# Blocked inverses in a gated-delta encoder: rows of 16 by substitution, one more level by products, and the heads' pieces placed anew

## The chip, the core and the metric

One Trainium2 chip, one of its cores. The metric is the device time of one execution, in microseconds (us), as the median of several runs. TensorE (PE) multiplies, VectorE (DVE), ScalarE (ACT) and GpSimd (POOL) do the elementwise work, and SyncE (SP) issues nearly all DMAs. Each engine takes its own instructions in the order in which the program queued them.

## What is computed

A layer of an encoder on 512 tokens of width 1024. Its input projection has 72 blocks of 128 columns and a small one. Eight heads of width 128 go through a gated delta rule, forwards and backwards, in chunks of 64 tokens (the kernel takes 128 tokens with the same result). What concerns the change is the inverse of a unit lower triangular matrix for each chunk and the lengths of q:

```python
q = _l2norm(q.reshape(bsz, t, N_HEADS, HEAD_DIM)) * (HEAD_DIM ** -0.5)
...
lmat = jnp.where(strict, jnp.einsum('nbhcd,nbhsd->nbhcs', kb, k) * decay, 0.0)
eye = jnp.eye(CHUNK, dtype=lmat.dtype)
tmat = lax.linalg.triangular_solve(lmat + eye, jnp.broadcast_to(eye, lmat.shape),
                                   left_side=True, lower=True, unit_diagonal=True)
u = jnp.einsum('nbhcs,nbhsd->nbhcd', tmat, v * beta[..., None])
w = jnp.einsum('nbhcs,nbhsd->nbhcd', tmat, kb * jnp.exp(gc)[..., None])
```

Then come a scan over the chunks, a norm and gate of its output, a short convolution branch, output projections, a layer norm, a feed-forward part (1024 to 4096 and back) and a second layer norm.

## The kernel before

All large products are made three times in fp32r (high by high, high by low, low by high), so each weight block is split first: ACT copies the high part (L122), DVE subtracts it for the low part (L118).

**Slots.** The middle of the kernel (L735 to L762) is nine slots. A slot is a run of block steps; one block step is three 128x512 products of a projection (L156 to L158), and eight of them are a block. Slots 0 to 8 have 88, 48, 48, 48, 48, 48, 40, 40 and 8 block steps. Between the block steps the pieces of three heads are queued: the scan of head h-1 (`scan_end`, at the block steps in FAR), the second part of head h's local work (`local`, at MID, in slot 0 MID0) and the first part of head h+1's (at BEGIN, in slot 0 BEGIN1; head 0 itself at BEGIN0). A negative number in BEGIN counts from the slot's end. A piece runs from one `yield` to the next. Within a block step the order is scan, second part, first part, then the three products. CONV, SC and Z tell after how many steps the convolution's copy, its two taps (L344, L345) and its silu are queued. PE, DVE, ACT and POOL keep this order exactly; DMAs on SP are placed by the framework's own ordering.

**A head's local work** (`gdn_local`, L423): `grow`, the running sums of the decay, is fetched; eight DVE instructions (L431) and two exponentials (L434, L435) make the decay; DVE scales it (L446); ACT and DVE split q and k (L451, L453). POOL squares q (L457, `q2`) and multiplies q into the decay (L460). DVE transposes `q2` in blocks of 32 (L465), adds it up (L467), and five small DMAs (L469, L472) with one more reduction (L543) bring the squared lengths of q onto the tokens. PE makes the score products `pg` (L481) and DVE multiplies in the decay (L485); ACT and DVE cut out the diagonal blocks of 32 (L495, L496), `dg`. Those go to DRAM (`xd`, L499) and back, spread by rows over four partitions: four DMAs for `Nb` (L503), four for `X` (L505). PE transposes v (`pv`, L511), POOL scales it.

**The substitution** (L520 to L536) runs on POOL alone: two instructions fold each second row into its neighbour (L526, L527), then 15 steps of one product (L532) and two sums (L535), and the identity is added (L536). Four DMAs write `xo` (L538), one reads it back as `U` (L542). DVE and ACT lay out the 32-blocks' inverses (`mt`, L549 to L552), and `level` (L554) makes from them the inverses of 64 and of 128: two rounds of small products on 32x32 or 64x64 tiles of the array (`pxa`, `pya`, `pxb`, `pyb`, L563 and L575) with copies by ACT and DVE between them.

Products of the projections take turns in two PSUM banks ("m"). A block's bank comes free when DVE has done both taps on it.

## Time and profile before

| | us |
|---|---|
| median of 3 runs | 1095.07 (1091.77 to 1096.57) |
| span of the profiled execution | 1085.6 |
| median less that span | 9.5 |
| PE, DVE, ACT, POOL busy | 1021.6, 543.5, 443.5, 393.0 |
| 0 to 31.1: loads, first block, gates | 31.1 |
| slot 0 / slot 1 / slots 2 to 5 | 87.4 / 48.2 / 220.9 |
| slot 6 / slot 7 | 49.9 / 42.8 |
| slot 8 and all that follows it | 605.3 |

The profiler's execution has no time of its own beside its span. What lies around the span is taken as the 9.5 us by which the median exceeds it. A slot's ends are the starts of its first and of the next slot's first 128x512 product. Slots 1, 2, 3 and 4 begin at 118.5, 166.7, 221.3 and 275.5 us.

In a row on a stretch the first number after its ends is its length; busy us (with instructions) of PE, PEld, DVE, ACT and POOL follow, then the granted clock of TensorE as a share of 2.4 GHz (it has two levels, 1.2 and 2.4 GHz, so 0.93 is full speed for 86% of the stretch), the DMA engines' busy share and GB/s. The other rows name an instruction by the engine, the line of the kernel and the tile that it writes. "Idle before" is how long its engine stood still just ahead of it, and what ended that.

### The profile page before, as it was taken

To read this page: it belongs to the slowest core of one execution; us is meant where nothing else is said; L and a number is where in the kernel's file an instruction comes from. 1 tells how busy PE (TensorE), PEld (TensorE's weight loads), DVE (VectorE), ACT (ScalarE), POOL (GpSimd) and SP (SyncE) were. 2 spreads that over 40 slices of the span, in tenths; PEclk is the share of its full clock that TensorE was granted. 3 is DMA by queue.
4 is the path that set the end of the run, shared out by engine and by line. 5 is a ranking of instruction groups with operands and counts; after the bars stand their busy time and mean duration, and the time that the engine had idled before them with its cause. 6 is when DMAs were issued, how large, how long until landed. Compare 5 with 4: busy or idle time off the path is not lost.

```text
span 1085.6 us, 14685 instructions
## 1 busy us (share of the span) xinstructions
PE 1021.6 (94%) x5523; PEld 843.0 (78%) x5523; DVE 543.5 (50%) x919; ACT 443.5 (41%) x804; POOL 393.0 (36%) x702
## 2 busy tenths in 40 slices
PE   9798999898979797999999999989999999999996
PEld 6576878686858686878888888879888888888885
DVE  6694686676666666353322246491222233333336
ACT  5652556464636364362434233222333343323231
POOL 1156757575656566740132012064222220000005
PEclk9899999898989898999999999999999999999998
DMA  6432243333323332222326324312322333232312
GB/s 207 116 93 68 87 96 100 83 93 78 99 69 108 69 107 75 82 88 78 98 98 225 102 83 152 117 47 90 98 97 95 99 116 114 86 106 87 106 48 77
DMA packets 77750, 106.84 MB, mean 98 GB/s; under 512 B 44336, under 2 KB 53104, under 8 KB 77680
## 3 DMA queue, kind: packets, MB, share of 16 engines
q1 hardware_dynamic: 77248, 105.26, 31.9%
q8 instruction: 43, 0.70, 0.3%
q10 hardware_dynamic: 432, 0.66, 0.2%
q14 instruction: 27, 0.22, 0.1%
HBM read 101.60 MB, written 4.29 MB: 98 GB/s over the span
## 4 chain that ended last, share of the span: by engine, by line
PE 56%; POOL 15%; DVE 12%; DMA 9%; issue 4%; SPq 3%; ACT 1%; POOLq 0%; DVEq 0%
PE accd L862 16%; POOL X L535 8%; PE ps_up L157 5%; POOL xt L532 5%; PE ps_up L158 5%; PE ps_up L156 5%; PE ps_in L156 4%; PE ps_in L158 4%; PE ps_in L157 4%; PE acco L862 3%; DMA xd<-dg 2%; DMA U<-xo 2%; DMA Nb<-xd 1%; PE psup L909 1%; DVE wl_in L118 1%
## 5 line engine op out<-in xcount | busy, mean ns | idle before, releaser
L156 PE MATMUL ps_in<-xh,wh_in 128*128 128x512 f32 x576 | 241.4, 419 | 22.0 <-DVE y L345 16.7
L158 PE MATMUL ps_in<-xh,wl_in 128*128 128x512 f32 x576 | 230.4, 400 | 4.2 <-DVE wl_in L118 4.2
L157 PE MATMUL ps_in<-xl,wh_in 128*128 128x512 f32 x576 | 229.5, 398 | 0.0
L156 PEld LDWEIGHTS ps_in<-xh,wh_in 128*128 128x128 f32 x576 | 111.4, 193 | 44.2 <-issue 18.3
L158 PEld LDWEIGHTS ps_in<-xh,wl_in 128*128 128x128 f32 x576 | 110.7, 192 | 31.9 <-DVE wl_in L118 7.7
L118 DVE TENSOR_TENSOR wl_in<-raw_in,wh_in 128x1024 fp32r<-128x1024 f32 x70 | 92.3, 1318 | 81.9 <-ACT wh_in L122 77.5
L157 PEld LDWEIGHTS ps_in<-xl,wh_in 128*128 128x128 f32 x576 | 111.6, 194 | 18.5 <-issue 0.3
L122 ACT ACTIVATE wh_in<-raw_in 128x1024 fp32r<-128x1024 f32 x70 | 73.9, 1055 | 64.8 <-PE ps_in L157 55.9
L862 PE MATMUL accd<-wh_down,hh 128*128 128x512 f32 x256 | 99.6, 390 | 0.0
L862 PE MATMUL accd<-wh_down,hl 128*128 128x512 f32 x256 | 99.4, 389 | 0.0
L862 PE MATMUL accd<-wl_down,hh 128*128 128x512 f32 x256 | 99.4, 389 | 0.0
L118 DVE TENSOR_TENSOR wl_up<-raw_up,wh_up 128x1024 fp32r<-128x1024 f32 x30 | 36.8, 1225 | 121.5 <-ACT wh_up L122 121.5
L535 POOL TENSOR_TENSOR X<-X,xt 128x60 f32<-128x60 f32 (+10 forms) x240 | 88.4, 368 | 18.8
L916 POOL TENSOR_TENSOR hf<-r 128x512 f32<-128x512 f32 x32 | 46.3, 1447 | 118.6 <-ACT r L914 118.6
L156 PE MATMUL ps_up<-x1h,wh_up 128*128 128x512 f32 x224 | 87.1, 389 | 0.0
L157 PE MATMUL ps_up<-x1l,wh_up 128*128 128x512 f32 x224 | 87.1, 389 | 0.0
L158 PE MATMUL ps_up<-x1h,wl_up 128*128 128x512 f32 x224 | 87.1, 389 | 0.0
L122 ACT ACTIVATE wh_up<-raw_up 128x1024 fp32r<-128x1024 f32 x30 | 31.8, 1060 | 106.3 <-PE ps_up L157 98.7
L966 POOL TENSOR_TENSOR xs<-xs,ln_g 128x1024 f32<-128x1024 f32 (+2 forms) x4 | 7.0, 1749 | 164.9 <-ACT xs L965 164.9
L104 DVE TENSOR_TENSOR wl_down<-raw_down,wh_down 128x1024 fp32r<-128x1024 f32 x32 | 40.0, 1253 | 50.4 <-ACT wh_down L103 48.8
L532 POOL TENSOR_TENSOR xt<-X,Nb 128x120 f32<-128x120 f32 (+10 forms) x120 | 58.4, 487 | 9.3
L862 PEld LDWEIGHTS accd<-wh_down,hh 128*128 128x128 f32 x256 | 48.0, 188 | 10.4 <-ACT wh_down L103 0.4
(256 smaller groups left out, 1922.3 us busy)
## 6 DMA issues: line engine op xcount, KB each, us to landing
...
```

Of the source, the lines that this page charges most:

```text
L104: (lo_eng or nc.vector).tensor_tensor(out=lo, in0=src, in1=hi.bitcast(F32), op=ALU.subtract)
L118: (nc.gpsimd if pool else nc.vector).tensor_tensor(out=wl, in0=raw, in1=wh.bitcast(F32), op=ALU.subtract)
L122: act(out=wh, in_=raw, func=AF.Copy)
L156: nc.tensor.matmul(acc, wh[:, c], mh[k], start=(k == 0), stop=False)
L157: nc.tensor.matmul(acc, wh[:, c], ml[k], start=False, stop=False)
L158: nc.tensor.matmul(acc, wl[:, c], mh[k], start=False, stop=(k == KT - 1))
L532: sub(out=t, in0=X[:, 0:r, k:k + 2].unsqueeze(3).broadcast_to([Q, r, 2, n]), in1=Nb[:, k:k + 2, k + 1:32].unsqueeze(1).broadcast_to([Q, r, ...
L535: sub(out=X[:, 0:r, k + 1:32], in0=X[:, 0:r, k + 1:32], in1=t[:, :, m], op=ALU.add)
L862: nc.tensor.matmul(acc[:, o], a[:, ts_], b[:, hs], start=start and j == 0, stop=stop and j == 2, skip_group_check=True)
L909: nc.tensor.matmul(acc[:, ts_], a[:, c], b[k][:, ts_], start=(k == 0 and t2 == 0 and j == 0), stop=(k == KT - 1 and t2 == 1 and j == 2), s ...
L916: nc.gpsimd.tensor_tensor(out=hfl, in0=r, in1=r, op=ALU.mult)
L966: nc.gpsimd.tensor_tensor(out=y[:, js], in0=y[:, js], in1=lnc["g"][:, js], op=ALU.mult)
```

## The change

The substitution goes on blocks of 16 instead of 32. Sixty-four blocks of 16 per head are spread over 128 partitions, two to a block. `X` starts from the identity by a copy on POOL (`eye`, loaded once) instead of four DMAs; the steps are eight, on at most 16 columns, in two pieces instead of sixteen. `xo` is two fixed DRAM tiles that are zeroed once. A new level on TensorE makes the 32-blocks' inverses: `UT` on DVE, 32 products 32x32 (`px0`), a copy on ACT (`lx0`), 32 products (`py0`), and one DVE instruction that adds their right half where the mask `uppr` is one. The squares of q are made by ACT, and their sums by four products with a column of ones (`pl`) in the piece of v's transposes; the DVE transposes and reductions and the five DMAs for them go. All lists of places are new.

```diff
-BEGIN0 = (5, 6, 7, 8, 8, 9, 11, 12, 15, 15, 16, 18, 18, 20, 24, 24)
-KEYS0 = 7
-BEGIN = (0, 0, 0, 4, 5, 5, 16, 20, 21, 22, 22, -17, -15, -14, -9, -6)
+BEGIN0 = (4, 10, 11, 11, 11, 18, 18, 18, 18, 18, 20, 20, 20, 21, 22)
+KEYS0 = 2
+BEGIN = (0, 6, 6, 6, 6, 6, 16, 21, 22, 26, -9, -7, -4, -4, -4)
-BEGIN1 = (20, 26, 27, 30, 30, 31, 31, 36, 39, 41, 43, 58, 62, 62, 71, 76)
+BEGIN1 = (20, 22, 22, 24, 28, 30, 30, 30, 34, 40, 59, 62, 62, 70, 81)
-MID = (2, 2, 4, 4, 5, 5, 6, 9, 10, 10, 12, 12, 14, 17, 18, 20, 20, 31, 33, 33, 35, 39, 43)
-MID0 = (42, 42, 45, 46, 46, 47, 47, 47, 50, 55, 57, 57, 59, 60, 61, 61, 65, 76, 81, 83, 84, 87, 88)
-FAR = (2, 2, 4, 5, 8, 9, 11, 11, 13, 14, 15, 18, 22, 23, 23, 25, 37)
+MID = (0, 7, 14, 19, 22, 24, 27, 28, 28, 32, 36, 41)
+MID0 = (31, 31, 41, 54, 55, 55, 57, 57, 58, 59, 64, 67)
+FAR = (1, 3, 4, 4, 7, 8, 10, 10, 13, 14, 15, 18, 22, 23, 31, 31, 43)
-CONV = ((2, 2, 3), (0, 2, 2), (0, 2, 2), (4, 5, 3))
-SC = (5, 3, 5)
-Z = (7, 8)
+CONV = ((0, 2, 3), (1, 2, 2), (0, 2, 2), (4, 5, 2))
+SC = (2, 3, 6)
+Z = (3, 8)
...
-    dadd = cons.tile([32 * RG, 32 // RG, 32], F32, name="dadd")
-    nc.sync.dma_start(out=dadd, in_=diag)
+    dm16 = cons.tile([P, 16], F32, name="dm16")
+    nc.vector.tensor_tensor(out=dm16, in0=dmask[:, 0:16], in1=dmask[:, 16:32], op=ALU.mult)
...
+    eye = cons.tile([P, 8, 16], F32, name="eye")
+    for g in range(2):
+        for t in range(2):
+            nc.sync.dma_start(out=eye.rearrange("(b g) (s t) j -> g t b s j", g=2, t=2)[g, t],
+                              in_=diag[2 * t + g, 0:4, 0:16].partition_broadcast(P // 2))
+    zero = gnear.tile([P, 256], F32, tag="lx32", name="zero", bufs=1)
+    nc.gpsimd.memset(zero, 0.0)
+    xos = [dram.tile([8, 4, 32, 32], F32, name=f"xo{i}") for i in range(2)]
+    for xo in xos:
+        nc.sync.dma_start(out=xo.rearrange("x a i j -> (x a i j)").rearrange("(p f) -> p f", p=P), in_=zero)
...
-        nc.gpsimd.tensor_tensor(out=q2, in0=qk[:, 1, :], in1=qk[:, 1, :], op=ALU.mult)
+        act(out=q2, in_=qk[:, 1, :], func=AF.Square)
...
-        q2t = gnear.tile([P, NT], F32, tag="lx", name=f"q2t{h}", bufs=2)
-        nc.vector.transpose(out=q2t, in_=q2)
-        sq4 = gdn.tile([P, 4, NCH], F32, tag="sq4", name=f"sq4{h}", bufs=2)
-        nc.vector.tensor_reduce(out=sq4, in_=q2t.rearrange("p (c b f) -> p b c f", b=4, f=32), axis=AX.X, op=ALU.add)
-        sqd = dram.tile([4, 32, 4, NCH], F32, tag="sqd", name=f"sqd{h}", bufs=2)
-        nc.sync.dma_start(out=sqd.rearrange("a t b c -> (a t) b c"), in_=sq4)
-        sqp = gdn.tile([P, 4, NCH], F32, tag="sqp", name=f"sqp{h}", bufs=2)
-        for b in range(4):
-            nc.sync.dma_start(out=sqp[32 * b:32 * b + 32], in_=sqd.rearrange("a t b c -> b t a c")[b])
...
+        dc = gnear.tile([P, 8, 16], F32, tag="dc", name=f"dc{h}", bufs=2)
+        stt(out=dc, in0=dgf[:, :, 16:32], scalar=lowr, in1=dgf[:, :, 0:16], op0=ALU.mult, op1=ALU.add)
+        tt(out=dc, in0=dc, in1=dm16.unsqueeze(1).broadcast_to([P, 8, 16]), op=ALU.mult)
+        nc.sync.dma_start(out=xd.rearrange("x a i j -> (a i) x j"), in_=dc)
...
+        for g in range(2):
+            nc.sync.dma_start(out=Nb.rearrange("(b g) i j -> g b (i j)", g=2)[g],
                               in_=xd.rearrange("x a i j -> (x a) (i j)"))
-            nc.sync.dma_start(out=X.rearrange("(b g) r j -> g b r j", g=RG)[g],
-                              in_=xd.rearrange("x a (r g) j -> g (x a) r j", g=RG)[g])
...
+        pl = ps("l", f"pl{h}")
+        for c in range(NCH):
+            nc.tensor.matmul(pl[:, c:c + 1], q2[:, c * P:(c + 1) * P], ones[:, 0:1], start=True, stop=True)
+        nc.vector.tensor_scalar(out=ss[:, 1], in0=pl[:, 0:NCH], scalar1=1e-6, scalar2=None, op0=ALU.add)
...
+        nc.gpsimd.tensor_copy(out=X, in_=eye)
...
+        sub(out=t, in0=along.unsqueeze(2).broadcast_to([P, 7, 16]), in1=Nb[:, 1:14:2, :], op=ALU.mult)
+        sub(out=Nb[:, 0:13:2, :], in0=Nb[:, 0:13:2, :], in1=t, op=ALU.add)
+        for k in range(0, 16, 2):
+            if k == 6:
+                yield
+            n, r = 15 - k, k // 2 + 1
+            t = tmp[:, :r * 2 * n].rearrange("p (i m j) -> p i m j", m=2, j=n)
+            sub(out=t, in0=X[:, 0:r, k:k + 2].unsqueeze(3).broadcast_to([P, r, 2, n]),
+                in1=Nb[:, k:k + 2, k + 1:16].unsqueeze(1).broadcast_to([P, r, 2, n]), op=ALU.mult)
             for m in range(2):
-                sub(out=X[:, 0:r, k + 1:32], in0=X[:, 0:r, k + 1:32], in1=t[:, :, m], op=ALU.add)
-        sub(out=X, in0=X, in1=dadd, op=ALU.add)
...
+                sub(out=X[:, 0:r, k + 1:16], in0=X[:, 0:r, k + 1:16], in1=t[:, :, m], op=ALU.add)
+        for s_ in range(2):
+            for g in range(2):
+                o = slice(16 * s_, 16 * s_ + 16)
+                nc.sync.dma_start(out=xo[:, :, o, o].rearrange("x a (r g) j -> g (x a) r j", g=2)[g],
+                                  in_=X.rearrange("(b s g) r j -> s g b r j", s=2, g=2)[s_, g])
...
+        nc.vector.transpose(out=UT.rearrange("p x j -> p (x j)"), in_=Uf.rearrange("p x j -> p (x j)"))
+        yield
+        px_ = ps("l", f"px0_{h}")
...
+        for x_ in range(8):
+            for a in range(4):
+                q = slice(32 * a, 32 * a + 32)
+                nc.tensor.matmul(pxv[q, x_, :], dgf[q, x_, :], UT[q, x_, :], start=True, stop=True)
+        lx0 = gnear.tile([P, 8, 32], F32, tag="lx0", name=f"lx0_{h}", bufs=1)
+        act(out=lx0, in_=pxv, func=AF.Copy)
+        yield
+        py_ = ps("l", f"py0_{h}")
...
+                nc.tensor.matmul(pyv[q, x_, :], lx0[q, x_, :], Uf[q, x_, :], start=True, stop=True)
+        stt(out=Uf[:, :, 16:32], in0=pyv[:, :, 16:32], scalar=uppr, in1=Uf[:, :, 16:32], op0=ALU.mult, op1=ALU.add)
+        yield
```

In the new lists the second part of a head begins with the substitution: first half (MID 0), second half and `xo` (7), `U` (14), `UT` (19), `px0` (22), `py0` (24), `mt` (27), `pxa` (28), the diagonals (28), `pya` (32), `pxb` (36), `pyb` (41). In BEGIN the decay's five pieces stand at 6, the split of q and k at 21 and 22, the squares and q's decay at 26, the scores at 39 and 41, and `dc` with `xd`, v with `pl`, and v's scaling at 44 of 48.

## Rows read from the trace of the kernel before

**Rows 1.** The page: busy time of TensorE and its weight loads, share, instructions.
```profile
PE 1021.6 (94%) x5523; PEld 843.0 (78%) x5523; DVE 543.5 (50%) x919; ACT 443.5 (41%) x804; POOL 393.0 (36%) x702
```

**Rows 2.** Stretches (slots 0, 1, 2-5, 6, 7, rest): length, busy by engine, PEclk, DMA.
```profile
31.10:118.50 87.40, 72.39 (x403) 57.62 (x401) 56.65 (x109) 39.85 (x71) 43.39 (x81) 0.92 0.37 97
118.50:166.70 48.20, 46.77 (x336) 39.17 (x333) 37.64 (x83) 29.28 (x68) 33.13 (x76) 1.00 0.32 84
166.70:387.60 220.90, 198.82 (x1329) 162.77 (x1329) 143.87 (x312) 117.39 (x264) 134.76 (x309) 0.93 0.33 87
387.60:437.50 49.90, 43.47 (x310) 35.52 (x309) 33.47 (x73) 26.78 (x61) 32.04 (x77) 0.93 0.33 93
437.50:480.30 42.80, 40.22 (x291) 33.16 (x289) 17.69 (x36) 17.84 (x44) 30.29 (x66) 0.96 0.27 80
480.30:1076.00 595.70, 591.54 (x2746) 493.29 (x2744) 227.43 (x246) 193.62 (x269) 110.71 (x76) 1.00 0.30 100
```

**Rows 3.** Waits of TensorE: for whom, us in total, times, longest us.
```profile
PE ps_in L156 <- DVE y L345: 16.7, 4, 5.4
PE pxa L563 <- DVE mt L549: 11.8, 6, 5.8
PE pv L511 <- ACT y L360: 5.6, 1, 5.6
PE ps_in L156 <- ACT wh_in L122: 5.2, 1, 5.2
PE ps_in L158 <- DVE wl_in L118: 4.2, 3, 2.4
```

**Rows 4.** Waits of VectorE: the one for q's squares.
```profile
DVE q2t L465 <- POOL q L457: 32.2, 5, 7.9
```

**Rows 5.** Timeline of VectorE: start us, us, instruction, idle before it.
```profile
198.11 0.71 DVE L465 STREAM_TRANSPOSE q2t<-q 128x512 f32<-128x512 f32 x1 [6.29 <-POOL q L457]
...
225.68 3.10 DVE L431 SCALAR_TENSOR_TENSOR dec<-grow,gc,madd 128x128 f32<-128x128 f32 x4
...
258.62 0.30 DVE L549 STREAM_TRANSPOSE mt<-U 32x128 f32<-32x128 f32 x1 [1.27 <-DMA U<-xo]
```

**Rows 6.** Timeline of GpSimd in slot 3: the substitution's start and end.
```profile
225.62 1.02 POOL L526 TENSOR_TENSOR xt<-Nb 128x480 f32<-128x480 f32 x1 [4.46 <-DMA Nb<-xd]
...
248.32 0.30 POOL L532 TENSOR_TENSOR xt<-X,Nb 128x56 f32<-128x56 f32 x1
248.70 0.56 POOL L535 TENSOR_TENSOR X<-X,xt 128x28 f32<-128x28 f32 x2
...
250.29 0.74 POOL L536 TENSOR_TENSOR X<-X,dadd 128x256 f32<-128x256 f32 x1
```

**Rows 7.** Timeline of ScalarE in slot 3: the decay's exponential.
```profile
228.81 1.06 ACT L434 ACTIVATE dec<-dec 128x1024 f32<-128x1024 f32 x1 [1.48 <-DVE dec L431]
```

**Rows 8.** Timeline of SyncE's issues, from the end of slot 2 on.
```profile
215.01 0.38 SPq L499 DMA_DIRECT2D xd<-dg  x1
218.99 0.49 SPq L503 DMA_DIRECT2D Nb<-xd  x1
...
251.06 2.52 SPq L538 DMA_DIRECT2D xo<-X  x4
```

**Rows 9.** Timeline of TensorE: small products in slots 2 and 3, and what follows them.
```profile
209.16 0.45 PE L575 MATMUL pya<-na,lxa 32*32 32x32 f32 x32
209.54 0.50 PE L156 MATMUL ps_in<-xh,wh_in 128*128 128x512 f32 x1
...
245.79 0.61 PE L642 MATMUL po<-vh,na 128*128 128x128 f32 x4
246.15 0.47 PE L156 MATMUL ps_in<-xh,wh_in 128*128 128x512 f32 x1
```

**Rows 10.** Timelines in slot 0: VectorE's wait, TensorE's stall.
```profile
42.67 2.19 DVE L431 SCALAR_TENSOR_TENSOR dec<-grow,gc,madd 128x128 f32<-128x128 f32 x8 [8.07 <-DMA grow<-gcd]
...
47.90 0.79 PE L156 MATMUL ps_in<-xh,wh_in 128*128 128x512 f32 x1 [5.18 <-ACT wh_in L122]
```

More of the change, by code (lines that the diff above doesn't have):

```diff
@@ L226 @@
         nc.vector.tensor_scalar(out=dmask[q], in0=ident[q, q], scalar1=-1.0, scalar2=1.0, op0=ALU.mult, op1=ALU.add)
-    dadd = cons.tile([32 * RG, 32 // RG, 32], F32, name="dadd")
-    nc.sync.dma_start(out=dadd, in_=diag)
+    dm16 = cons.tile([P, 16], F32, name="dm16")
+    nc.vector.tensor_tensor(out=dm16, in0=dmask[:, 0:16], in1=dmask[:, 16:32], op=ALU.mult)
+    lowr = cons.tile([P, 1], F32, name="lowr")
+    nc.vector.tensor_reduce(out=lowr, in_=dmask[:, 16:32], axis=AX.X, op=ALU.add)
+    nc.vector.tensor_scalar(out=lowr, in0=lowr, scalar1=-1.0, scalar2=16.0, op0=ALU.mult, op1=ALU.add)
+    uppr = cons.tile([P, 1], F32, name="uppr")
+    nc.vector.tensor_scalar(out=uppr, in0=lowr, scalar1=-1.0, scalar2=1.0, op0=ALU.mult, op1=ALU.add)
     cwq = cons.tile([P, 24, 3], F32, name="cwq")
@@ L528, in gdn_local @@
-        for k in range(1, 31, 2):
-            yield
-            n, r = 31 - k, (k + RG) // RG
+        sub = nc.gpsimd.tensor_tensor
+        nc.gpsimd.tensor_copy(out=X, in_=eye)
+        tmp = gnear.tile([P, 128], F32, tag="xt", name=f"xt{h}", bufs=1)
+        t = tmp[:, :7 * 16].rearrange("p (m j) -> p m j", j=16)
+        along = Nb.rearrange("p i j -> p (i j)")[:, 1:1 + 34 * 6 + 1:34]
+        sub(out=t, in0=along.unsqueeze(2).broadcast_to([P, 7, 16]), in1=Nb[:, 1:14:2, :], op=ALU.mult)
@@ L534, in gdn_local @@
             for m in range(2):
-                sub(out=X[:, 0:r, k + 1:32], in0=X[:, 0:r, k + 1:32], in1=t[:, :, m], op=ALU.add)
-        sub(out=X, in0=X, in1=dadd, op=ALU.add)
-        for g in range(RG):
-            nc.sync.dma_start(out=xo.rearrange("x a (r g) j -> g (x a) r j", g=RG)[g],
-                              in_=X.rearrange("(b g) r j -> g b r j", g=RG)[g])
+                sub(out=X[:, 0:r, k + 1:16], in0=X[:, 0:r, k + 1:16], in1=t[:, :, m], op=ALU.add)
+        xo = xos[h % 2]
@@ L542, in gdn_local @@
         nc.sync.dma_start(out=U.rearrange("p d c j -> p (d c) j"), in_=xo.rearrange("x a i j -> (a i) x j"))
-        nc.vector.tensor_reduce(out=ss[:, 1, :], in_=sqp.rearrange("p a c -> p c a"), axis=AX.X, op=ALU.add)
-        nc.vector.tensor_scalar(out=ss[:, 1], in0=ss[:, 1], scalar1=1e-6, scalar2=None, op0=ALU.add)
+        yield
+        Uf = U.rearrange("p d c j -> p (d c) j")
+        UT = gnear.tile([P, 8, 32], F32, tag="UT", name=f"UT{h}", bufs=1)
+        nc.vector.transpose(out=UT.rearrange("p x j -> p (x j)"), in_=Uf.rearrange("p x j -> p (x j)"))
+        yield
+        px_ = ps("l", f"px0_{h}")
+        pxv = px_[:, :256].rearrange("p (x t) -> p x t", t=32)
+        for x_ in range(8):
[6 more added lines that the diff above has]
+        py_ = ps("l", f"py0_{h}")
+        pyv = py_[:, :256].rearrange("p (x t) -> p x t", t=32)
+        for x_ in range(8):
+            for a in range(4):
+                q = slice(32 * a, 32 * a + 32)
+                nc.tensor.matmul(pyv[q, x_, :], lx0[q, x_, :], Uf[q, x_, :], start=True, stop=True)
+        stt(out=Uf[:, :, 16:32], in0=pyv[:, :, 16:32], scalar=uppr, in1=Uf[:, :, 16:32], op0=ALU.mult, op1=ALU.add)
         yield
```

22 lines of the change are left out of this document (3 added, 19 removed).

## The prediction

> **What bounds the kernel now.** I read the page first: TensorE is busy for 94% of the span [rows 1], so only its idle time, its slow stretches and its own work can move the end. Busy time by stretch comes next: from 480.3 us to 1076 TensorE is busy 591.5 of 595.7 us at full clock, and the change has nothing there. It is in slots 0 to 7 that TensorE both waits and runs at the lower level: slots 2 to 5 hold 198.8 busy us in 220.9, at a mean clock of 0.93, while slot 1 holds 46.8 in 48.2 at 1.00 [rows 2]. Slots 1 to 5 have the same work, so slot 1 tells what a slot costs with hardly a stall: 48.2 less its idle 1.4 is 46.8 us. Four such slots are 187; slots 2 to 5 lose 34 us.
>
> The waits say to what. The largest is for the second tap of a convolution on VectorE, which frees a PSUM bank: 16.7 us in four waits; 5.6 more before `pv` are the same in slot 6, one step on, by way of the silu [rows 3]. VectorE was late since it stood still itself: for `q2`, the squares of q on GpSimd, 32.2 us in five waits [rows 4]. In slot 2 it waits 6.29 us with the taps queued behind [rows 5]. GpSimd's square is queued behind the whole substitution, which in slot 3 runs from 225.62, when `Nb` lands, to 251.03 [rows 6], 25.4 us. After each of these stalls the clock falls. Of the 34 us that slots 2 to 5 lose, 22 are idle time (220.9 less 198.8); the other 12 are work done at the lower level, and the mean of 0.93 bears that out: 31 us at half speed, a part of them idle [rows 2].
>
> **The change part by part.**
>
> *q's lengths.* The square leaves GpSimd for ScalarE, and VectorE's transpose of it is gone. The stall of rows 4 cannot come from there: 22.3 us of TensorE's waits go (16.7 and 5.6), and with them the clock's falls. ScalarE gets two more instructions a head, the square and later `lx0`, together about 1 us (the square has half the elements of a decay exponential, which at 1.06 us is the nearest row on ScalarE [rows 7]). ScalarE is busy 117 of 220.9 us [rows 2], and that idle time hides them; if `vh` of the scan is queued right behind one, it costs that slot up to 1 us. VectorE loses a transpose and two reductions and gets `dc`, `UT`, and one instruction on `py0`: even. It is busy 144 of 220.9 us. On SP five DMAs a head go, and with them the wait for the first of the five to land.
>
> *Products with ones.* Four products with 128 columns of weights and one moving column, each two instructions in fp32, eight in all. No row has one column. From above: the four instructions with 128 moving columns from 245.79 to 246.15 [rows 9] are 0.09 us each, so 0.72. From below: eight at the 0.012 of a 32-wide one (next paragraph), 0.1; a gain is excluded, since TensorE had no such work. The weights are as many as in the first row, which is the nearer, so I take 0.8 with a change of shape; at the lower end the eight heads together are 5 us less.
>
> *The new level.* `px0` and `py0` are 32 products each, 64 instructions. `pya` has 32 of the same size and kind: from 209.16 to 209.54, 0.38 us [rows 9], 0.012 each with the turn of shape. So 64 take 0.76, with the turn back 0.9; two are 1.8. Together a head pays 2.6 us on TensorE, which nothing hides, 21 us for eight. The row has four tiles of the array in turn, and 12 ns from one instruction to the next. Against this part speaks a rule of the Trainium skill (TensorE: Matmul & The Clock Gate, Part 1): however small a matmul is, the next one starts no sooner than about 25 ns after it. By that page of the Trainium skill the estimate for 64 would be 1.6 us, and the end some 13 us later than by the row; the trace does not agree with it for `pya`.
>
> *The substitution.* A pair step of the old one at the size of the new ones (56 and 28 elements) takes 0.30 and 0.56 us with a pause of 0.08 behind each (248.62 to 248.70), 1.02 [rows 6]. Eight are 8.2, the fold and the copy of `eye` some 1.2: 9.4 us. VectorE works beside it, and its L431 shows what that costs: 0.27 us each quiet in row 42.67 [rows 10], 0.78 in row 225.68 [rows 5]. I take 9.4 to 12 us against 25.4.
>
> *The new chain in a slot.* The scores now stand at 39 and 41 and `dc` at 44 of 48, so `xd` is issued about 3 us before the slot ends, where it was 6.3 (215.01 against 221.3). `Nb` came 4.0 us after `xd`'s issue and started landing for the substitution at 225.62, as the last of eight DMAs. Now there are two: 4.0 and some 3 for issue and landing put it at +4, against +4.3. The substitution ends at +13.5 to +16. From its end to `U` were 7.6 us (251.03 to 258.62) [rows 5, 6, 8]; the same four DMAs out and one in: `U` lands at +21 to +24. `UT` takes VectorE at most 0.7 (the transpose of twice the columns [rows 5]). TensorE reaches `px0` at about +23.8: step 23 began at 246.15, +24.9 of slot 3, less one step and one small product [rows 9]. So `px0` waits 0 to 1 us. Behind VectorE's wait for `U` stands only the low part of the next block's weights, wanted at step 24. I give a slot 1.5 us of stalls in all: 1 here and at `pxa`, 0.5 where the scan's R is late.
>
> *Sum by slots.* Slots 2 to 5: 46.8 + 2.6 + 1.5 = 50.9 each, 203.6 against 220.9: -17.3. Slot 1, which had no stall to lose: 50.9 against 48.2, +2.7. Slot 6 has eight steps fewer, 5.5 us: 45.4 against 49.9, -4.5. Slot 7 has no next head: 42.8 less its idle 2.6 (busy 40.2) and 1.7 of clock (0.96 is 3.4 us at half speed) is 38.5 [rows 2]; plus 1.8 and 1.5: 41.8, -1.0. Slot 0: it is idle for 15.0 us (87.4 less 72.4), of which 5.2 are for the weights' high part, 5.8 for `mt` and nearly all the rest for the low part [rows 2, 3]. Its clock of 0.92 over 87.4 us is 14 us at the lower level, 6 of them idle, so 4 lost. 87.4 - 19 = 68.4. It pays for two heads' ones and one level, 3.4. The first stall stays in part: VectorE stood still until 42.67 for `grow`, and ScalarE's exponentials behind it held the weights until 47.90 [rows 10]. The exponentials move from step 9 to 18, but the eight decay instructions (2.2 us) and then the low part of the weights (1.2) still come after `grow`, so TensorE goes on at about 46: 3 us of stall instead of 7.6. `px0` and `py0` both stand at 55 with ScalarE's copy between, 1 us, and `U` comes near its step: 2 more; clock 2.5. 68.4 + 3.4 + 8.5 = 80.3: -7.1. At the start four small instructions on VectorE and six DMAs on SP are new, +0.5. The sum is -26.7, a span of 1058.9; with 9.5 around it, by which the median shown exceeds the span shown, 1068.4.
>
> **Rivals.** *U late (slower).* If `U` lands later than +23, VectorE stands still with it and TensorE waits at `px0`, in order, with all projections behind it. The point from which it decides is some 3 us, where the rows show the clock falling too. SP may do that: it takes its issues in order, and weight loads set ahead of `xo` or `U` cost issue and traffic; or the substitution, beside VectorE, takes 15 us. Price at 4.5 us of wait and 2.7 of clock: a slot is 46.8 + 2.6 + 7.2 = 56.6. Slots 2 to 5 +5.5, slot 1 +8.4, slot 6 +1.2, slot 7 +4.7, slot 0 -4: +15.8, so 1111. For it: the slack is 1 to 2 us. Against it: the substitution is 14 us shorter and SP has fewer issues to get through.
>
> *The burst at step 6 (same).* All eight decay instructions now come at one step and the exponentials (1.06 us each [rows 7]) right behind. Beside the substitution they are 0.78 us each [rows 5], 6.2 us; R and `vh` of the scan, at steps 7 to 10, stand behind them. At 3 us of stall and 2.7 of clock a slot is 55.6 or so: slots 2 to 5 +1.5, slot 1 +7, slot 6 0, slot 7 -1, slot 0 -7: about 1096. Against it: VectorE can start on them before TensorE is at step 6.
>
> *Small products at half the pace (faster, less).* The new products use the four tiles on the array's diagonal, eight deep each; `pya` crosses tiles and is four deep. Should each wait for the one before it on its tile, so that the distance is twice that of `pya`, 0.024 us, the 64 take 1.5 instead of 0.76: 1.5 a head, 12 in all, 1080. Against it: `pya` too has only four tiles in turn. The Trainium skill's page named above would put the distance there.
>
> *No stall at all (faster, more).* 1.5 less in seven slots and 6 in slot 0: 1052.
>
> **How the numbers follow.** A measurement of this kernel tells about 0.5% (5.5 us) from no change, so the same is 1089.6 to 1100.5. My sum, 1055 to 1079: 0.55. No stall: 0.08. Slow small products: 0.05. The burst: 0.16, a third of it below 1089.6. `U` late: 0.16. That is faster 0.73, same 0.11, slower 0.16. The time is 1068. For 8 in 10 I leave out half of the last case and part of the no-stall case: 1050 to 1100.
>
> **What would show it.** Right: no wait of VectorE on GpSimd for `q2`, no wait of TensorE on L345's taps in slots 2 to 6; the substitution from `Nb` to its last sum in 9.4 to 12 us; `px0` and `py0` some 0.9 us each; the eight `pl` instructions in 0.8; clock 1.00 in slots 1 to 6; slots 1 to 5 near 51 us. Wrong: `px0` waiting on `UT` for 3 us or more; TensorE's scan products waiting on R or `vh` near step 8; slots 1 to 5 above 54.

## The result, and the profile after

The changed kernel takes 1076.2 us (1074.2 to 1077.2) against 1093.4 us of the kernel before beside it: a ratio of 0.985, with an interval from 0.982 to 0.988. The profiled span is 1072.5 us against 1085.6. So it is faster by some 17 us, 13 of them in the profiled spans, where the forecast had 27. The time lies inside the range, and the sign is right; half of the gain in the spans is missing, and the profile tells in which places. Each timed run of the changed kernel is 1.7 us longer than its own span (1074.17 against 1072.5 in the profiled one), not 9.5; what that does to the forecast is said below.

Two parts of the page first: the busy time of the engines, which answers to [rows 1], and a queue that brings instructions (queue and kind: packets, MB, share).

```profile
PE 1034.5 (96%) x6611; PEld 853.3 (80%) x6611; DVE 531.2 (50%) x923; ACT 452.6 (42%) x820; POOL 284.3 (27%) x527
...
q8 instruction: 52, 0.85, 0.3%
```

TensorE has 1088 instructions more than before, 136 a head (64 each for the 32 products of `px0` and of `py0`, 8 for the four of `pl`), and GpSimd 109 us of work less. The stretches that answer to [rows 2] are slots 0, 1, 2, 3, 4 and 5, 6, 7 and the rest (start and end, length, busy us and instructions of PE, PEld, DVE, ACT, POOL, clock, DMA share, GB/s):

```profile
33.10:120.00 86.90, 77.14 (x546) 62.40 (x545) 53.87 (x108) 42.62 (x76) 27.27 (x64) 0.92 0.31 89
120.00:172.90 52.90, 50.55 (x469) 42.15 (x468) 35.04 (x78) 29.32 (x68) 15.25 (x41) 0.97 0.30 82
172.90:222.10 49.20, 48.90 (x469) 40.96 (x469) 34.70 (x79) 30.69 (x69) 20.50 (x56) 1.00 0.30 84
222.10:278.80 56.70, 50.52 (x469) 42.12 (x468) 35.36 (x79) 30.61 (x69) 20.10 (x55) 0.94 0.33 73
278.80:377.40 98.60, 97.88 (x937) 81.94 (x936) 71.06 (x156) 61.29 (x137) 40.81 (x110) 1.00 0.32 84
377.40:421.60 44.20, 43.66 (x445) 36.56 (x444) 33.10 (x77) 27.15 (x63) 20.12 (x59) 1.00 0.27 70
421.60:462.10 40.50, 40.48 (x418) 33.20 (x418) 15.54 (x37) 18.42 (x46) 21.20 (x49) 1.00 0.27 73
462.10:1063.00 600.90, 596.93 (x2744) 493.00 (x2742) 225.79 (x246) 194.06 (x269) 111.17 (x77) 1.00 0.32 99
```

The marks between these slots stand at the second product of a slot, 0.2 to 0.3 us behind the first (slot 0 starts at 32.8, slot 3 at 221.9, the rest at 461.8). Slots 2, 4 and 5 are at 49.2 and 98.6 for two, with the clock at 1.00 and hardly any idle time: better than the 50.9 forecast. Slot 3, with the same 469 matmul records, takes 56.7 at a clock of 0.94. Slot 1 is at 52.9 with 0.97, slot 0 at 86.9 instead of 80.3. And the rest, from 462.1 to the end at 1072.5, is 610.4 us where it was 605.3 (1085.6 less 480.3), though the diff has nothing there. The waits of TensorE (for whom, us in all, times, longest), which answer to [rows 3]:

```profile
PE py L577 <- issue: 6.6, 2, 6.2
...
PE px L568 <- DVE UT L561: 3.5, 3, 3.0
PE pxa L597 <- issue: 3.1, 2, 2.4
PE pg L488 <- ACT qh L468: 2.3, 1, 2.3
PE pg L488 <- DVE ql L470: 2.3, 1, 2.3
```

The taps and `mt` are gone from it, and so is VectorE's wait for `q2` [rows 3, 4]. What stands there instead is of two kinds: waits in slot 0 (`pg`, and the 3.0 us of `px0`), and a new one, "issue", inside runs of small products, with nothing that the profile names as the cause. The largest, in slot 3 (timelines of GpSimd, SyncE, VectorE and TensorE, in this order, which answer to [rows 6, 8, 5, 9]):

```profile
226.43 0.46 POOL L537 TENSOR_TENSOR xt<-Nb 128x112 f32<-128x112 f32 x1 [0.19 <-DMA Nb<-xd]
...
236.58 0.50 POOL L547 TENSOR_TENSOR X<-X,xt 128x8 f32<-128x8 f32 x2
```

```profile
237.11 2.61 SPq L552 DMA_DIRECT2D xo<-X  x4
...
241.71 0.53 SPq L107 DMA_DIRECT2D raw_in<-in_w_in  x1
242.33 0.38 SPq L443 DMA_DIRECT2D grow<-gcd  x1
```

```profile
243.75 0.45 DVE L561 STREAM_TRANSPOSE UT<-U 128x256 f32<-128x256 f32 x1 [0.41 <-DMA U<-xo]
```

```profile
244.68 0.75 PE L568 MATMUL px<-UT,dg 32*32 32x32 f32 x64
245.36 0.50 PE L155 MATMUL ps_in<-xh,wh_in 128*128 128x512 f32 x1
...
247.40 0.72 PE L577 MATMUL py<-U,lx 32*32 32x32 f32 x60
254.30 0.32 PE L577 MATMUL py<-U,lx 32*32 32x32 f32 x4 [6.18 <-issue]
```

The chain is as forecast: the substitution runs from 226.4 to 237.1, 10.7 us, `UT` is done at 244.2, and `px0` starts without a wait. Then TensorE stops for 6.18 us after 60 of the 64 instructions of `py0`. All its operands are there, since the first 60 read the same tiles. The clock falls while it stands still: the granted clock is 0.72 over the stop and 0.94 on the slot's mean, the only one of slots 2 to 5 below 1.00.

### The profile page after: what moved, and what is told of

It is laid out like the page before. It is cut to its first block, busy times and chain, and to the rows that moved or that the text cites. A ratio compares the mean times of both kernels' runs of the same rounds, so it can differ in the third digit from the quotient of the medians.

```text
span 1072.5 us, 16601 instructions
## 1 busy us (share of the span) xinstructions
PE 1034.5 (96%) x6611; PEld 853.3 (80%) x6611; DVE 531.2 (50%) x923; ACT 452.6 (42%) x820; POOL 284.3 (27%) x527
## 4 chain that ended last, share of the span: by engine, by line
PE 84%; DVE 5%; DMA 3%; POOL 3%; issue 2%; ACT 1%; SPq 1%; POOLq 0%; DVEq 0%; ACTq 0%
PE accd L896 16%; PE ps_in L155 11%; PE ps_in L157 10%; PE ps_in L156 10%; PE ps_up L156 5%; PE ps_up L155 5%; PE ps_up L157 5%; PE acco L896 3%; POOL X L547 2%; PE psup L943 1%; PE ps_osc L155 1%; PE ps_osc L157 1%; PE ps_osc L156 1%; PE ps_ogd L157 1%; PE ps_ogd L155 1%
## 5 line engine op out<-in xcount | busy, mean ns | idle before, releaser
L157 PE MATMUL ps_in<-xh,wl_in 128*128 128x512 f32 x576 | 227.0, 394 | 1.8 <-DVE wl_in L117 1.8
L156 PE MATMUL ps_in<-xl,wh_in 128*128 128x512 f32 x576 | 227.1, 394 | 0.0
L117 DVE TENSOR_TENSOR wl_in<-raw_in,wh_in 128x1024 fp32r<-128x1024 f32 x70 | 96.9, 1384 | 87.0 <-ACT wh_in L121 86.4
L121 ACT ACTIVATE wh_in<-raw_in 128x1024 fp32r<-128x1024 f32 x70 | 74.0, 1057 | 71.0 <-PE ps_in L156 52.9
L121 ACT ACTIVATE wh_up<-raw_up 128x1024 fp32r<-128x1024 f32 x30 | 31.8, 1060 | 106.2 <-PE ps_up L156 98.6
L103 DVE TENSOR_TENSOR wl_down<-raw_down,wh_down 128x1024 fp32r<-128x1024 f32 x32 | 40.0, 1253 | 52.4 <-ACT wh_down L102 50.9
L896 PEld LDWEIGHTS accd<-wh_down,hl 128*128 128x128 f32 x256 | 48.1, 188 | 11.6
L896 PEld LDWEIGHTS accd<-wl_down,hh 128*128 128x128 f32 x256 | 48.1, 188 | 11.6
L102 ACT ACTIVATE wh_down<-raw_down 128x1024 fp32r<-128x1024 f32 x32 | 33.7, 1053 | 52.9 <-PE accd L896 52.5
```

The lines of the kernel that those rows point to most:

```text
L102: act(out=hi, in_=src, func=AF.Copy)
L103: (lo_eng or nc.vector).tensor_tensor(out=lo, in0=src, in1=hi.bitcast(F32), op=ALU.subtract)
L117: (nc.gpsimd if pool else nc.vector).tensor_tensor(out=wl, in0=raw, in1=wh.bitcast(F32), op=ALU.subtract)
L121: act(out=wh, in_=raw, func=AF.Copy)
L156: nc.tensor.matmul(acc, wh[:, c], ml[k], start=False, stop=False)
L157: nc.tensor.matmul(acc, wl[:, c], mh[k], start=False, stop=(k == KT - 1))
```

## The experiments

**The stop and the instruction loads.** The DMA view of slot 3 up to 251.8 us, and of the 2.5 us behind it (queue and kind: packets, MB, share of the 16 engines):

```profile
q1 hardware_dynamic: 3695, 2.08, 40.2%
...
q1 hardware_dynamic: 119, 0.34, 35.7%
q8 instruction: 1, 0.02, 2.4%
```

For 29.7 us no instructions come in; then one load does, and TensorE goes on at 254.3. If I count every record of TensorE's queue in the trace from its start, its semaphore instructions too, the four stops fall at records 1985, 3777, 4801 and 6593: all are 193 above a multiple of 256. And 52 loads for some 13,300 records are one for 256. The Trainium skill (Runtime: NRT & Kernel Launch, section Instruction fetch mechanics) says that an engine's instructions come in blocks of 16 KiB, 256 instructions each, ahead of their use; the trace agrees (0.85 MB in 52 loads). It also says that crossing into the next block is mostly hidden. Here it is not: from 244.5 to 248.1 us TensorE went through 270 records, more than a block, and the load that ended the stop started only at 251.9.

The first test moves nothing but the place of these boundaries.

```diff
-    for i in range(10):
+    for i in range(7):
         nc.tensor.matmul(warm[:, :P], ones, ones, start=True, stop=True)
+    for i in range(51):
+        q = slice(32 * (i % 4), 32 * (i % 4) + 32)
+        nc.tensor.matmul(warm[q, :32], ones[q, 0:32], ones[q, 0:32], start=True, stop=True)
```

> The changed kernel, but of the ten 128-column products that warm TensorE up at the very start three are replaced by 51 products of 32x32, which makes its instruction stream longer by 192 ahead of everything else; all else is the same. Theory (code loading): the four stalls that the changed kernel's trace puts down to issue (slot 1 pxa 2.35 us, slot 3 py 6.18, slot 4 pxa 0.72, slot 6 py 0.37) begin with the matmul or weight load number 1985, 3777, 4801 and 6593 of the stream, which all leave 193 when divided by 256: TensorE runs out of loaded instructions there. Shifted by 192 the same places come to lie inside other work: the stalls of 6.2 and 2.35 us go, slot 3 falls from 56.7 to 49-50 us and slot 1 from 53.0 to 50-51; where one is left, it is again at a number that leaves 193 (slot 2 and slot 5 inside the 32x32 products are the candidates). Time 1064-1070 us against 1076. Rival (the stall belongs to the py products of slot 3, to a transfer of their data, or to the clock): it stays in slot 3 with about 6 us, time 1075-1077.

Measured: 1067.7 us, a ratio of 0.979 [0.977, 0.981]. Slots 1 and 3 of this kernel, and where its one stop lies in TensorE's timeline:

```profile
120.60:169.60 49.00, 49.00 (x469) 41.04 (x468) 35.11 (x79) 29.41 (x68) 16.20 (x42) 1.00 0.35 89
...
220.20:272.90 52.70, 50.42 (x469) 42.03 (x468) 35.51 (x79) 30.64 (x69) 19.43 (x56) 0.97 0.30 79
```

```profile
249.29 0.20 PE L600 MATMUL pxa<-U,na 32*32 32x32 f32 x3
251.78 0.26 PE L600 MATMUL pxa<-mt,na 32*32 32x32 f32 x1 [2.28 <-issue]
```

The stops of 6.2 and 2.4 us are gone; slot 1 is at 49.0. A new one of 2.28 us stands in slot 3, not in `py0` now but in `pxa`, at record 4033, again 193 above a multiple of 256. The time is inside the expected range. I had looked for a stop that is left in slot 2 or 5, so the place was a miss and the number a hit. The stop belongs to the count of instructions, not to `py0`: the theory holds, the rival falls.

The second test leaves the boundaries and moves a transfer: `grow`, which goes out when its buffer comes free, beside `U` and `px0`, is held until step 33 by a memset of one column.

```diff
+    def load_grow(h, held=False):
+        grow = gdn.tile([P, 2 * NCH, P], F32, tag="grow", name=f"grow{h}", bufs=3)
+        if held:
+            nc.vector.memset(grow[:, 0, 0:1], 0.0)
+        nc.sync.dma_start(out=grow, in_=gcd_v[h].partition_broadcast(P))
+        return grow
...
+                if 1 <= h < NH - 2 and u == GROW_AT:
+                    grows[h + 2] = load_grow(h + 2, True)
```

> The changed kernel, but the 512 KB transfer of grow is allocated in the slot before and held until step 33 of it by a one-column memset on VectorE, so that it no longer goes out beside U and the first 32x32 products (242.3 us in slot 3). Theory (instruction loads queue behind data): in slot 3 the load that starts at 251.9 us is behind raw_in and grow, issued at 241.7 and 242.3; without grow it starts several us earlier and the stall of 6.2 us falls under 3; time 1069-1073 us. Rival 1 (the load is asked for late, whatever else moves): 6 us stay, 1076 us. Rival 2 (grow itself comes too late for the dec operations of the next slot): new VectorE waits on grow in slots 2 to 6 and 1076 us or more.

Measured: 1063.3 us, 0.974 [0.972, 0.977], more than expected. Its slots 1 and 2 to 5, and the DMA view of slot 3 up to 246.5 us:

```profile
123.20:172.10 48.90, 48.90 (x470) 40.94 (x470) 35.16 (x79) 29.43 (x68) 16.42 (x42) 1.00 0.33 90
172.10:368.00 195.90, 195.38 (x1874) 163.70 (x1873) 141.22 (x316) 122.58 (x273) 81.78 (x221) 1.00 0.33 85
```

```profile
q8 instruction: 1, 0.02, 0.2%
```

The load is there before 246.5 us (it starts at 244.9, where it started at 251.9), and the stops in slots 1 to 5 are gone; one of 0.3 us is left in slot 6. Five slots in a row take 244.8 us, 49.0 each, at full clock with half a microsecond idle. So the load was late because `grow` went out when it did. Whether it stood behind `grow`'s packets on a DMA engine or somewhere else on the way isn't shown. Rival 2 fell too: nothing waits for `grow`.

**The 5 us behind the slots.** The mean time of a product of the last layer in the kernel before and after (out<-in, count, busy us, mean ns; 768 such products in three groups, of which one is shown):

```profile
L862 PE MATMUL accd<-wh_down,hh 128*128 128x512 f32 x256 | 99.6, 390 | 0.0
```

```profile
L896 PE MATMUL accd<-wh_down,hh 128*128 128x512 f32 x256 | 101.0, 395 | 0.0
```

By the sizes in the code the constants of the changed kernel are 384 bytes a partition smaller (`dadd` is gone, `eye` and the masks are new), so everything behind them lies 384 bytes lower; the last layer's weights, allocated from the other end, stay where they were. That is read from the code; no trace has addresses.

```diff
+    pad = cons.tile([P, 96], F32, name="pad")
+    nc.gpsimd.memset(pad[:, 0:1], 0.0)
```

> The changed kernel with one unused tile of 96 columns (384 bytes a partition) among the constants, so that the weights and activations lie at the addresses that they had in the kernel before. Theory (addresses): in the part of the kernel that the diff doesn't touch, the products of the last layer take 395 ns each in the changed kernel's trace where they took 390 before, and three products 1.4 us more in every thousand for that alone; with the old addresses they go back to 390, the part behind the last slot from 610 to about 605 us, and the kernel from 1076 to 1070-1071 us. Rival (another chip, or the layer's own transfers): 395 ns and 1076 us stay. On the stalls nothing should change under either: about 6 us inside the py products of slot 3 and about 2 us inside the pxa products of slot 1, since TensorE's order of instructions is the same.

Measured: 1073.4 us, 0.984 [0.982, 0.986], where the expectation had 1070 to 1071. The product and the last stretch:

```profile
L898 PE MATMUL accd<-wh_down,hh 128*128 128x512 f32 x256 | 99.6, 390 | 0.0
```

```profile
463.80:1060.00 596.20, 591.63 (x2744) 492.96 (x2742) 226.46 (x246) 194.09 (x269) 111.25 (x77) 1.00 0.32 100
```

The products are back at 390 ns, and from the last slot's start to the end it is 605.6 us (1069.4 less 463.8) instead of 610.4. In all other runs the mean goes the same way: 393 to 398 ns in the changed kernel's variants without the unused columns, 389 or 390 in those with 88 or 96 of them and in the kernel before with one part of the change. The theory holds for its place. Yet the total falls within the error of the changed kernel's, since the start and slots 0 to 7 took nearly 1 us more each in this profile: the stops are at the same records (1985, 3777, 4801, and one of 1.84 us in slot 0 at 961, also 193 above a multiple of 256), but of other lengths, 1.85, 4.93 and 1.97 us. Between these two kernels a stop's length varies; its place doesn't. Why 384 bytes make a product slower isn't shown, only that the size of the constants decides it.

**Slot 0.** The step of mine that failed here concerned the exponentials. ScalarE in the changed kernel's slot 0:

```profile
46.56 0.69 ACT L357 ACTIVATE y<-ps_in,cwq 128x512 f32<-128x512 f32 x1 [3.21 <-PE ps_in L157]
...
48.56 1.06 ACT L451 ACTIVATE dec<-dec 128x1024 f32<-128x1024 f32 x1
...
50.47 1.04 ACT L468 ACTIVATE qh<-y 128x1024 fp32r<-128x1024 f32 x1
```

At step 18 they stand behind the convolution's middle, which waits for TensorE until 46.56 us, and a load of ScalarE's function table, 1.28 us from 47.27, comes first; `qh` is done at 51.5, and `pg` waits for it. With the exponentials moved ahead of the convolution's middle:

```diff
-BEGIN0 = (4, 10, 11, 11, 11, 18, 18, 18, 18, 18, 20, 20, 20, 21, 22)
+BEGIN0 = (4, 10, 11, 11, 11, 14, 14, 14, 15, 15, 20, 20, 20, 21, 22)
```

> The changed kernel with five entries of slot 0's list changed: the exponentials and the decay at step 14 instead of 18, qh at 14, ql and q's squares at 15, the pg products at step 20 as they are. Theory (my price for slot 0 failed because the exponentials stand on ScalarE behind the convolution's middle, which waits for TensorE until 46.56 us): TensorE's two waits at pg (2.3 us for qh, 2.3 us for ql) go, the inverse's chain of head 0 starts some 2-3 us earlier, its 3.0 us wait of px0 on UT shrinks under 1, and the two low stretches of the clock at 52.8 and 87.0 us go with them; slot 0 from 86.9 to 77-81 us, time 1066-1071 us. Rival (the convolution's middle and its silu, which now stand behind the exponentials, hold up the projections or pv by as much): slot 0 at 85-88, 1075-1078 us.

Measured: 1072.5 us, 0.984 [0.981, 0.986]: no gain that can be told from the changed kernel's 0.985, and a time between the two ranges; slot 0 takes 86.1 us. The waits of TensorE:

```profile
PE px L568 <- DVE UT L561: 5.9, 2, 5.6
...
PE pv L518 <- DVE na L492: 1.7, 1, 1.7
```

Both waits at `pg`, 4.6 us, are gone but for 0.2. `px0` waits 5.6 instead of 3.0: TensorE came earlier, `U` hardly (`UT` at 85.81 against 86.40). So the rival holds, by another way than the one that I wrote down: the wait moved to the next late thing. One reason that `U` is late in slot 0 is that the substitution takes longer there, in the changed kernel 14.2 us (65.7 to 79.9) against 10.7 in slot 3. Beside VectorE's instructions with two inputs single GpSimd instructions take about three to four times as long. One product of the substitution takes 0.27 us in slot 3 (at 235.30); in slot 0 it stands beside the split of a weight block (76.19 to 77.46):

```profile
76.46 1.13 POOL L544 TENSOR_TENSOR xt<-X,Nb 128x42 f32<-128x42 f32 x1
```

That agrees with the Trainium skill (SBUF — State Buffer, section Who interferes with whom): a VectorE instruction with two inputs in SBUF contends with a GpSimd instruction that reads SBUF.

**One part of the change alone: q's lengths.** The kernel before, with the squares on ScalarE and the products with ones, and its 32-row substitution and its placing as they were.

```diff
-        nc.gpsimd.tensor_tensor(out=q2, in0=qk[:, 1, :], in1=qk[:, 1, :], op=ALU.mult)
+        act(out=q2, in_=qk[:, 1, :], func=AF.Square)
...
+        pl = ps("l", f"pl{h}")
+        for c in range(NCH):
+            nc.tensor.matmul(pl[:, c:c + 1], q2[:, c * P:(c + 1) * P], ones[:, 0:1], start=True, stop=True)
```

> The kernel before with one part of the change alone: q's squares by ScalarE and their sums by four products with a column of ones in the step of v's transposes; the 32-row substitution and the placing of the steps stay (one entry is dropped from each list, as one step is gone). Theory (two causes stand one behind the other): VectorE's waits for GpSimd's squares (32.2 us in five) and TensorE's 3 to 5 us stalls before the projections in slots 2 to 5 go, but the chain of the inverse still takes the same time from the end of a slot: U lands 36 us after a slot's start (257.5 less 221.3 in slot 3), while pxa would now be reached some 31 us after it; so TensorE waits 4-5 us at pxa in slots 2 to 5 instead, and the clock falls there: slots 53-55 us as before, 1086-1094 us. Rival (one cause is enough): slots 2 to 5 at 48-50 us each and 1068-1072 us.

Measured: 1076.0 us, 0.984 [0.982, 0.987]: as fast as the whole change, and between the two theories. Slots 2 to 5, 6 and 7, and the first wait of TensorE:

```profile
166.40:381.70 215.30, 200.72 (x1362) 165.86 (x1362) 142.59 (x301) 119.60 (x268) 136.93 (x304) 0.94 0.35 90
381.70:426.80 45.10, 43.47 (x318) 35.88 (x316) 32.56 (x69) 27.48 (x62) 33.09 (x78) 0.96 0.34 94
426.80:466.10 39.30, 38.58 (x291) 32.11 (x288) 15.09 (x34) 17.51 (x44) 29.21 (x65) 1.00 0.28 81
```

```profile
PE pxa L555 <- DVE mt L541: 18.0, 5, 5.2
```

For slots 2 to 5 the theory of two causes in a row is right: 215.3 us against 220.9, that is 53.8 a slot; the taps' waits are down to 0.8 us in all, and TensorE waits 2.4 to 4.1 us a slot at `pxa` for the long substitution instead. What I missed are slots 6 and 7, where the second cause doesn't bite: 45.1 and 39.3 against 49.9 and 42.8, 8.3 us. The miss, a time 10 us below the theory's range, is one of the sum.

**The other part alone.** The changed kernel with `grow` held back, but q's lengths in the old way.

```diff
-        act(out=q2, in_=qk[:, 1, :], func=AF.Square)
+        nc.gpsimd.tensor_tensor(out=q2, in0=qk[:, 1, :], in1=qk[:, 1, :], op=ALU.mult)
...
+        nc.vector.transpose(out=q2t, in_=q2)
...
+        nc.vector.tensor_reduce(out=sq4, in_=q2t.rearrange("p (c b f) -> p b c f", b=4, f=32), axis=AX.X, op=ALU.add)
```

> The changed kernel with grow held back, and with q's lengths as they were before the change (squares on GpSimd, transposed and summed on VectorE, sorted by two transfers): the substitution in blocks of 16, the new level and the new placing alone. To be compared with grow held back, 1063.3 us. Theory (what made q's squares costly was that they stood on GpSimd behind a 25 us substitution): with a substitution of 11 us GpSimd is free at the step of the squares, VectorE waits 1-2 us for them and nobody for VectorE; the products pl (0.8 us a head) are saved, slots 1 to 5 at 48.0-48.8 us, 1056-1063 us. Rival (the wait on the squares comes back): VectorE waits 3-6 us a head, the taps come late and TensorE stalls before the projections again, slots at 52-55 us and 1080-1090 us.

Measured: 1067.9 us, 0.978 [0.976, 0.979], against 0.974 with the products; the theory had 1056 to 1063 us. VectorE in slot 3 of this kernel:

```profile
251.91 0.70 DVE L488 STREAM_TRANSPOSE q2t<-q 128x512 f32<-128x512 f32 x1
252.64 0.69 DVE L490 TENSOR_REDUCE sq<-q2t 128x16 f32<-128x512 f32 x1
253.24 0.29 DVE L597 STREAM_TRANSPOSE mt<-U 32x128 f32<-32x128 f32 x1
```

In slots 1 to 7 VectorE waits for no squares any more: GpSimd has them ready when it comes to them. In slot 0 it waits once, 7.5 us. The rival falls but for slot 0, which takes 90.2 us. But the 1.3 us of transposing and summing stand in front of `mt`, and `pxa` waits up to 1.3 us for that; slots 2 to 5 are at 50.0 instead of 49.0, and the saving of `pl` is eaten. Only with both halves, and `grow` held back, are slots 2 to 5 at 49.0 us each.

**The price of the small products.** On `grow` held back, the sums in one pass with two columns of ones, on rounded squares, and `py0` with the 16 columns that are used.

```diff
-                nc.tensor.matmul(pyv[q, x_, :], lx0[q, x_, :], Uf[q, x_, :], start=True, stop=True)
+                nc.tensor.matmul(pyv[q, x_, 16:32], lx0[q, x_, :], Uf[q, x_, 16:32], start=True, stop=True)
```

> The changed kernel with grow held back, and with the new small products made smaller: the sums of q's squares as four products of one pass (rounded squares, two columns of ones) instead of four of two passes with one column, and py0 with the 16 columns that are used instead of 32. To be compared with grow held back, 1063.3 us. Theory (their price is what TensorE takes for them, since slots 1 to 5 wait for nothing else): pl from 0.8 to 0.4 us a head and py0 from 0.7 to 0.4, so 48.8 us a slot become 48.1-48.3 and the kernel 1057-1060 us. Rival (a product has a least time whatever its size, or the slots are set by something else): 48.8 and 1063 us.

Measured: 1059.3 us, 0.970 [0.968, 0.973], inside the expected range; slots 1, 3 and 4 take 48.4 to 48.5 us, slots 2 and 5, where `px0` waits again, 48.9 and 49.0. Four heads' worth of both, first with `grow` held back alone, then here (count | busy us, mean ns):

```profile
L530 PE MATMUL pl<-ones,q 128*128 128x1 f32 x32 | 3.8, 240 | 0.0
L584 PE MATMUL py<-U,lx 32*32 32x32 f32 x256 | 3.0, 194 | 0.0
```

```profile
L532 PE MATMUL pl<-ones,q 128*128 128x2 f32 x16 | 2.3, 250 | 0.0
L586 PE MATMUL py<-U,lx 32*32 32x16 f32 x256 | 2.9, 180 | 0.0
```

Half the instructions of `pl` save 0.38 us a head; half the columns of `py0` save 0.03. The theory holds for the first, the rival (a least time whatever the size) for the second, at 32 and 16 columns. The small products alone don't make the 4 us: slot 0, 1.9 us shorter, has a large part in them.

**Everything together.** `grow` held back, the 96 columns, slot 0's exponentials earlier, its `px0` six steps later, and the masks, `eye` and the zeros of `xo` made after the first head's projections.

```diff
-MID0 = (31, 31, 41, 54, 55, 55, 57, 57, 58, 59, 64, 67)
+MID0 = (31, 31, 41, 60, 61, 61, 63, 63, 64, 65, 70, 73)
```

> The changed kernel with everything that the earlier runs pointed to: grow held back, the 96 columns among the constants, slot 0's exponentials at step 14, its inverse's last steps six steps later (px0 at 61 instead of 55), the masks, eye and the zeros of xo made after the first head's projections instead of among the loads of the tokens. Worked out from grow held back (1063.3 us): 5 for the addresses, 4-5 for pg's two waits in slot 0, 4-5 for px0's wait on UT, 3 to 6 for the clock's two low stretches in slot 0, 1-2 at the start: 1042-1050 us. Rival (in slot 0 what is late there comes from the loads of the weights, so that the wait only moves): 1053-1058 us.

Measured: 1059.4 us, 0.970 [0.968, 0.971]. Against `grow` held back the span falls from 1062.6 to 1058.4: the part behind the slots gives 4.9, the start 2.0 (slot 0 begins at 31.4), and slot 0 takes 2.9 back, at 92.7. The time lies above both ranges. The sum for slot 0 failed again, and the rival of late weights is what SyncE's timeline shows:

```profile
62.67 0.33 SPq L108 DMA_DIRECT2D raw_in<-in_w_in  x1
78.35 2.61 SPq L542 DMA_DIRECT2D xo<-X  x4
...
82.84 6.93 SPq L108 DMA_DIRECT2D raw_in<-in_w_in  x4
```

For 15 us SyncE issues nothing, because `xo` waits for the substitution at the head of its queue, and the weights wait behind it. VectorE's `UT` then stands behind the split of such a late block.

```diff
-                nc.sync.dma_start(out=xo[:, :, o, o].rearrange("x a (r g) j -> g (x a) r j", g=2)[g],
+                nc.gpsimd.dma_start(out=xo[:, :, o, o].rearrange("x a (r g) j -> g (x a) r j", g=2)[g],
```

> The kernel best1 (1059.4 us) with one edit: the four transfers of xo are issued by GpSimd, right behind its substitution, instead of by SyncE. Theory (in slot 0 of best1 SyncE issues nothing from 62.7 to 78.35 us because xo waits there for GpSimd, so that the weights behind it start at 82.8 and later, TensorE waits 5.3 us at px0 behind UT behind a late split, 2.7 at pxa): a weight block goes out some 10 us earlier, both waits shrink to under 2 us together, two of the clock's three low stretches in slot 0 go, slot 0 from 92.7 to 80-84 us, 1047-1051 us. Rival (U itself is late in slot 0, the substitution ends at 78.3 whoever sends its result): px0 still waits 4-5 us, 1057-1060 us. A price to watch: GpSimd takes some tenths to one us for each transfer that it issues.

> As xo_pool, with the narrower small products as well (they gave 4 us beside grow held back). If both add up: 1043-1047 us; slots 1 to 5 at 48.4 us each. If a wait on UT takes the place of the time saved: 1047-1051 us.

Measured: `xo` from GpSimd 1057.1 us, 0.966 [0.964, 0.968]; with the narrower products 1053.1 us, 0.962 [0.960, 0.965], the fastest here and some 42 us below the kernel before beside it. The first time is the rival's, the second lies above both ranges. Of the expected gain in slot 0 only part came: `px0` waits 1.7 us instead of 5.3, `pxa` still 2.5, and slot 0 is at 88.9. `U` itself is fetched no sooner (at 82.80 against 82.36), as the rival had it; what went is the late split in front of `UT`. Slots 1 to 5 of `best2`:

```profile
119.40:361.90 242.50, 242.05 (x2321) 202.34 (x2320) 174.34 (x395) 152.06 (x339) 110.93 (x284) 1.00 0.32 86
```

They are now nothing but TensorE's work, 242.1 us in 242.5. In slot 0 one more stop at a block of instructions, 2.5 us at `pg` and again at record 961, is left. What slot 0 would take without its waits stays open; no edit here brought it below 86 us.

## Why the prediction was right, and where it was not

*What bounded the kernel: right.* The waits for the taps, `pv` and `mt` are gone [rows 3], and so is VectorE's wait on the squares [rows 4]; with q's lengths alone the taps' and the squares' waits go too, while those for `mt` rise from 11.8 to 18.0 us. The clock falls within these stalls and not after them: in slot 2 at 201.5 us, in the one that ends at 202.4.

*The chain: right in each of its steps.* `Nb` at +4.3 us of slot 3 (forecast +4), the substitution 10.7 us (9.4 to 12), its end at +15.0 (+13.5 to +16), `UT` at +21.7 (`U` +21 to +24), `px0` at +22.6 without a wait. The rival of a late `U` didn't happen in slots 1 to 7; in slot 0 it did. The burst at step 6 brought no wait for R or `vh`. Two of my signs of being wrong came all the same: `px0` waited 3.0 us, in slot 0, and slot 3 took more than 54 us, for a reason that I didn't have.

*The new work on TensorE: a little too dear.* `px0` to the next product is 0.68 us where I took 0.9. `pl` takes 0.81 to the next product, as forecast (0.8). A slot without a stall takes 48.9 us (`grow` held back), so a head costs 2.1 on the 46.8 of slot 1 before, not 2.6, and the 1.5 us of left-over stalls a slot weren't there: 49 instead of 50.9. The Trainium skill's 25 ns from one product to the next (TensorE: Matmul & The Clock Gate, Part 1) would have made 1.6 us of the 64; at 0.68 they are 11 ns apart, and the trace doesn't agree with it for products on four tiles in turn.

*The time was nearer than the span, by luck.* The span is 13.6 us above the forecast one, the time 7.8 (1076.2 against 1068.4). The difference is the 9.5 us that I put around the span. No run shows that term: each run's time exceeds its own span by 1.7 to 2.0 us, and in the changed kernel the median exceeds the profiled span by 3.7. Then the profiled execution of the kernel before took about 1087.3 us (1085.6 and 1.7, an estimate), less than any of its four timed runs (1088.9 to 1096.6): its rows show a quicker execution than the median that I forecast from. With 1.7 the forecast would have been 1060.6.

*What was missing, 13.6 us of span (1072.5 against 1058.9):*

- Slot 3, +5.8, and slot 1, +2.0: the stops at instruction loads. No rival of mine had it. I priced 1088 more instructions by their duration on the array and not by what has to be fetched for them. This error is hidden in the sum but is the largest single one: with the boundaries moved the span falls by 7.3 us (to 1065.2), with `grow` moved by 9.9 (to 1062.6). Slots 2, 4 and 5, which escaped it but for 0.7 us in slot 4, were 1.1 to 2.1 us better than forecast each, so that slots 2 to 5 together came out as forecast (204.5 against 203.6) for the wrong reason. The clock fell with less than the 3 us of standing still that I took: with the 2.4 us in slot 1 too (0.97 on that slot's mean).
- Slot 0, +6.6: TensorE stands still for 9.8 us of it where I had 6, and is busy for 5.3 us more than the 71.8 without stalls, where I had 2.5 for the clock. The weights' wait took 1.6 instead of 3, `px0` and `py0` 3.5 against 3, but `pg`, at which I had nothing, waited 4.6, and two stretches at the lower clock came with these waits (52.8 to 59.7 and 87.0 to 93.8 us). The step that failed is the first stall: I had it at the weights, with TensorE going on at about 46. It went on at 41.2 and stopped at `pg` instead, because the exponentials had been put behind a convolution that itself waits for TensorE.
- The rest, +5.1 (5.4 by the slot's first product): put at 0, since the diff has nothing there. Shown to come from the smaller constants; 4.4 of it are the 768 products of the last layer.
- The start, +1.5 over the 0.5 forecast (1.2 by the slot's first product): small instructions and six DMAs ahead of the tokens' work. Moved behind it (`best1`), slot 0 begins at 31.4 us, where it began at 31.1 before the change and at 32.8 after it.
- Slots 6 and 7, -1.2 and -1.3: no stalls there either.

*Where the gain comes from.* I took the two halves of the change as one cure. Each alone all but takes away TensorE's waits for the taps. With q's lengths alone, 1076.0 us, the long substitution decides instead; the whole, 1076.2, ends no earlier, as it has the stops at instruction loads. With `grow` held back the whole is at 1063.3 and the substitution's half alone at 1067.9, so that q's half is worth 4 to 5 us beside the other. q's lengths alone with `grow` held back was not run.
